# Row factor on VectorE, first low-rank split ahead of the key norm, token norm one unit later

## The chip, the cores and the metric

The kernel runs on one core of a Trainium2 chip. A core has a matrix engine (TensorE, PE in the profile; its weight loads are PEld), VectorE (DVE), ScalarE (ACT), GpSimd (POOL) and SyncE (SP), which here only issues transfers. Each takes its instructions in one order that is fixed when the program is built, and waits at an instruction until its semaphores are up. The metric is the device time of one execution in microseconds (us), as the median of several runs; lower is better. What is measured of this kernel without any change varies by some tenths of a per cent between runs.

## The reference, cut to what matters

One layer of a hybrid encoder in float32: 256 tokens, width 2048.

```python
u = rms_norm(x, norm_mix_pre)                # every token divided by its root mean square
proj = u @ w_in                              # q, k, v of two attentions, RWKV-7 inputs, gates
y_a = stick_breaking_attention(q_a, k_a, v_a)
y_b = forgetting_attention(q_b, k_b, v_b, log_f)
z = z + (z_prev - z) * mu                    # RWKV-7: token shift of the projected features
w_log = -softplus(-(w0 + tanh(wd) @ w_up)) - 0.5     # low-rank products with 64 rows
a = sigmoid(a0 + ad @ a_up)
kk = (k * k_k) / norm_of_each_head(k * k_k)          # the key norm
...                                          # recurrence over chunks of 64 tokens, group norm, gate
m = sum(sigmoid(gate_i) * (y_i @ P_i)); x = x + rms_norm(m @ w_out)
x = x + rms_norm(relu(rms_norm(x) @ w_mlp_up) ** 2 @ w_mlp_down)
```

The division by a token's root mean square is a factor per row of `u`, so `u @ w_in` may be formed without it and each result multiplied by the factor afterwards. The kernel does that.

## The kernel before, in words

**Weights.** All big weights lie in HBM as one stream of half-megabyte pieces. For each piece SP issues a transfer into a tile `raw` (three buffers); ACT copies it, rounded, to `whi` (L152); DVE subtracts to get the remainder `wlo` (L153). `wnext` keeps one piece ahead of the products (`AHEAD = 1`), and `whi` and `wlo` have three buffers each. A `raw` buffer comes free for the next transfer when DVE has made `wlo` from it.

**Units.** `unit(pks)` forms 128 columns of `u @ w_in` for all 256 tokens: two halves, each with eight products with `whi` (L168; the very last is L176) and eight with `wlo` (L172). The result stands in a PSUM bank in two parts. `evac` empties it: ACT copies one part (L227), DVE adds the other (L228). For RWKV features `shift` does the same with L585 and L586, and then mixes neighbouring tokens: ACT scales into `zp` (L588), DVE combines (L589). In `tok`, which forms 512 columns for 128 tokens at a time, the products are L198 and L214.

**The row factor.** `squares` sums the squares of the input into two tiles `a` (ACT L371, DVE L373). `norm` adds them over partitions with products with a matrix of ones (L378), and DVE and ACT make the factor `rstd` from that (L380, L241 to L246). `scaled(d)` multiplies a result by `rstd` (L395), in `evac`'s loop for the first eight units, after `evac` for the next eight, and inside `shift`. `turned_rstd` makes the same factor with tokens on partitions (L387 to L392).

**Mixers.** The attentions and RWKV run as generators between the products: a `yield` hands back control until a planned time of the written PE order has come, so their few products are written into PE's order at a planned place. PE's order is exactly this written one. The other engines' order is set by a scheduler when the program is built, from the order in which the code is written and what each instruction depends on; `pin` keeps one instruction where the code has it.

**Stick-breaking attention** (`sb_mix`) multiplies its logs by a mask on POOL (L448, two groups of four), ACT then rounds them (L454), and DVE takes the remainder (L455).

**RWKV, one half of the heads at a time** (`rwkv_half`): the squares of the keys (ACT L655, L660, DVE L661), sums per head on PE (L668), the inverse root (ACT L672, L675, DVE L670, L680 to L685; this is the key norm), then for each pair of heads `p` the low-rank products (PE L696). Their weights come through `lora_load(p)` (two transfers on ACT's queue, L639, into the one buffer `lor`) and `lora_split(p)` (ACT L645, then twice DVE L647, into the one tile `lows`).

In the second half of the heads the group norm and gate of the first half run at the same time (`gate_norm`: ACT L947, DVE L946, L948, L954, PE L952).

Of the kernel before, what the change touches and what calls it, by code (L numbers as in the profile page):

```python
# [12 lines left out]
AF = mybir.ActivationFunctionType  # L13
ALU = mybir.AluOpType
# [36 lines left out]
def hybrid_block(ctx, tc, xt, x, gains, params, consts, lora, gup, wst, out):  # L51
    nc = tc.nc
    V, A, G, PE = nc.vector, nc.scalar, nc.gpsimd, nc.tensor
# [11 lines left out]
    def nm(s):  # L65
        uid[0] += 1
        return f"{s}_{uid[0]}"
# [110 lines left out]
    def unit(pks):  # L178

        ps = gps()  # L180
        for h in range(2):
            hi, lo = wnext()
            gemm(ps, hi, lo, pks[8 * h:8 * h + 8], h == 0, h == 1, tick)
        return ps
# [37 lines left out]
    def pin(ins):  # L222
        return tc.keep_in_program_order(ins)

    def evac(ps, dst):
        b = tmp()
        A.activation(b, ps[:, T:2 * T], AF.Copy)  # L227
        V.tensor_tensor(dst, ps[:, 0:T], b, ALU.add)  # L228
# [25 lines left out]
    def g1(w=T):  # L254
        return rp.tile([128, T], F32, tag="g1", name=nm("g1"), bufs=20)
# [109 lines left out]
    rstd = rp.tile([128, T], F32, name="rstd1")  # L365
# [9 lines left out]
    def norm():  # L375
        ps = mps()
        for i in range(2):
            PE.matmul(ps[:, 0:T], C("ones"), A6[:, i, :], start=i == 0, stop=i == 1)  # L378
        ms, t = tmp(), tmp()
        V.tensor_scalar(ms, ps[:, 0:T], 1.0 / D, EPS, ALU.mult, ALU.add)  # L380
        rsqrt(rstd, ms, t)
        return ms

    def turned_rstd(ms):
        ps = mps()
        for tt in range(2):
            PE.matmul(ps[:, 4 * tt:4 * tt + 4], ms[0:4, tt * 128:tt * 128 + 128], C("ident", slice(0, 4), 0, 4),  # L387
                      start=tt == 0, stop=tt == 1)
        r8 = rt.rearrange("p a b -> p (a b)")
        V.tensor_copy(r8, ps[:, 0:8])  # L390
        G.tensor_tensor(r8, r8, cst[:, 2:3].to_broadcast([128, 8]), ALU.pow)
        V.tensor_scalar(rt[:, :, 1], rt[:, :, 0], 0.5, None, ALU.mult)  # L392

    def scaled(d):
        G.tensor_tensor(d, d, rstd[0:d.shape[0]], ALU.mult)  # L395

    for i in range(2):
        wsplit(wraw())
# [5 lines left out]
    for h in range(8):  # L404
        ps = qb[h] if h < 3 else unit(upk)
        qk.append(g1())
        evac(ps, qk[h])
        if h == 3:
            ms = norm()
        if h == 5:  # L410
            turned_rstd(ms)
        for i in range(h + 1) if h == 3 else [h] if h > 3 else []:
            scaled(qk[i])
    done["sbq"], done["sbk"] = qk[:4], qk[4:]

# [164 lines left out]
    def shift(ps, i, dst, n=128):  # L580

        b, t = tmp(), tmp()
        zp = rp.tile([128, T + 1], F32, tag="zp", name=nm("zp"), bufs=2)
        G.memset(zp[:, 0:1], 0.0)
        A.activation(b[0:n], ps[0:n, T:2 * T], AF.Copy)  # L585
        V.tensor_tensor(t[0:n], ps[0:n, 0:T], b[0:n], ALU.add)  # L586
        scaled(t[0:n])
        A.activation(zp[0:n, 1:T + 1], t[0:n], AF.Copy, scale=P("mu", i, slice(0, n)))  # L588
        V.scalar_tensor_tensor(dst, t[0:n], omu[0:n, i:i + 1], zp[0:n, 0:T], ALU.mult, ALU.add)  # L589
# [37 lines left out]
    def rwkv_half(hf):  # L627
        PR = range(4 * hf, 4 * hf + 4)
        xw, xa, wl = done["low"]
# [12 lines left out]
        def lora_split(p):  # L642
            if p in PR:
                raw = lor[p]
                pin(A.activation(wl, raw, AF.Copy))  # L645
                for i, r in enumerate((slice(64, 128), slice(0, 64))):
                    V.tensor_tensor(wl[r, i], raw[r, i], wl[r, i].bitcast(F32), ALU.subtract)  # L647

# [8 lines left out]
        for i2 in range(2):  # L657
            s = B6[:, 2 * i2:2 * i2 + 2, :]
            hl = [rp.tile([128, 2, T], F32R, tag="BK", name=nm("sqh"), bufs=8) for _ in range(2)]
            A.activation(hl[0], s, AF.Copy)  # L660
            V.tensor_tensor(hl[1], s, hl[0].bitcast(F32), ALU.subtract)  # L661
            sqh.append(hl)
        yield 3.8
        for i2 in range(2):
            ri = B6[:, 2 * i2:2 * i2 + 2, :]
# [20 lines left out]
            yield 3.0  # L686
        SC = rp.tile([128, 32, 128], F32, tag="SC", name=nm("SC"), bufs=1)
        At, Bt, Kt, bon = {}, {}, {}, {}
        lora_split(PR[0])
        ecol = rp.tile([128, 4, 4], F32, tag="ecol", name=nm("ecol"), bufs=2)  # L690
        for i, p in enumerate(PR):
            ps = mps()
# [41 lines left out]
            A.activation(kph, kp, AF.Copy)  # L734
            V.tensor_tensor(kpl, kp, kph.bitcast(F32), ALU.subtract)
            lora_split(p + 1)
            yield f"v{p}"
            v = done[f"v{p}"]
# [220 lines left out]
    def mixers():  # L959
        yield from sb_mix()  # L960
        yield from fox_mix()
        yield from rwkv_lora()
        for hf in range(2):
            yield from rwkv_half(hf)
# [36 lines left out]
    for s in ("q", "k"):  # L1001
        lst = []
        for h in range(4):
            ps = unit(upk)
            t = g1()
            evac(ps, t)
            scaled(t)
            lst.append(t)
        done["fox" + s] = lst
# [7 lines left out]
    for hf in range(2):  # L1017
        for s, mo in (("k", MU_K), ("r", MU_R), ("v", MU_V)):
            for p in range(4 * hf, 4 * hf + 4):
                ps = unit(upk)  # L1020
                d = g1()
# [634 lines left out]
```

## Time and profile before

| | us |
|---|---|
| median of 3 runs | 1519.44 |
| lowest, highest | 1519.37, 1525.15 |
| the profiled execution, its own time | 1523.08 |
| its span in the trace | 1521.3 |
| PE busy in it | 1489.9 |
| DVE, ACT, POOL busy in it | 1210.3, 937.7, 139.2 |

Times in the profile count from the start of the span. "Busy" is the time in which an engine has an instruction in work; behind a waiting instruction the profile names what ended the wait. The granted clock is the share of its full clock that PE was given, 1.00 or less, and stands in the views by stretches of time as PEclk. The profiled execution took 3.64 us more than the median of the runs.

The three stages that the change touches all lie in the first 545 us: the first eight units (to 58 us), the rest of the projections with the two attentions and the first half of RWKV (to 345 us), and the second half of RWKV (around 490 us). The feed-forward layer after that (about 840 us to the end) is not touched.

### The profile page before, as it was taken

The page shows a single profiled execution, that of the slowest core. Times are in us where ns is not written, and L with a number is a line of the kernel's source. Part 1 is how long each engine was busy: PE and PEld are TensorE (multiplying, and loading weights), DVE is VectorE, ACT ScalarE, POOL GpSimd, SP SyncE. Part 2 cuts the span into 40 slices and gives each one's busy share as a digit, 9 for nine tenths or more (in the row PEclk, how much of TensorE's full clock was granted, in tenths as well). Part 3 has the DMA queues.
Part 4 walks back from the last instruction along what each step waited for, and adds up shares of the span by engine and source line. Part 5 has one row for each costly group of instructions (what it writes and reads, how often), then busy time and mean ns, then how long its engine had stood idle before and what let it go on. Part 6 is the DMA issues. An engine that isn't in the chain of part 4 may idle for free.

```text
span 1521.3 us, 22774 instructions
## 1 busy us (share of the span) xinstructions
PE 1489.9 (98%) x8401; PEld 1253.3 (82%) x8401; DVE 1210.3 (80%) x1644; ACT 937.7 (62%) x1398; POOL 139.2 (9%) x203
## 2 busy tenths in 40 slices
PE   8999999999998999999999999999999999999997
PEld 7888887888777888778887888888888888888885
DVE  7566577779768789658655788989899999899986
ACT  7465666554557554565444676777677676676763
POOL 0232011320000100000000000000000000000000
PEclk9999999999999999999999999999999999999999
DMA  7545454444634545545695568788888888988874
GB/s 257 185 146 179 170 179 158 160 161 167 206 136 146 172 160 193 175 145 180 238 302 190 201 201 251 245 246 258 263 249 232 259 256 240 272 249 252 274 250 151
DMA packets 107616, 317.71 MB, mean 209 GB/s; under 512 B 10736, under 2 KB 14704, under 8 KB 107248
## 3 DMA queue, kind: packets, MB, share of 16 engines
q1 hardware_dynamic: 94832, 284.91, 54.4%
q0 software_dynamic: 8064, 29.36, 10.3%
q10 hardware_dynamic: 4608, 1.97, 0.5%
q8 instruction: 66, 1.08, 0.3%
q14 instruction: 46, 0.38, 0.1%
HBM read 282.65 MB, written 4.19 MB: 189 GB/s over the span
## 4 chain that ended last, share of the span: by engine, by line
PE 64%; DVE 2%; issue 1%; DMA 1%; ACT 1%; POOL 0%; POOLq 0%; DVEq 0%; ACTq 0%
PE gps L214 18%; PE gps L168 14%; PE gps L172 8%; PE gps L198 5%; PE mps L1386 3%; PE mps L1388 3%; PE mps L1387 3%; PE gps L1388 2%; PE gps L1386 2%; PE gps L1387 2%; PE gps L176 1%; DVE wlo L153 1%; DMA sp<-in_wst_dram 1%; PE mps L745 0%; ACT whi L152 0%
## 5 line engine op out<-in xcount | busy, mean ns | idle before, releaser
L153 DVE TENSOR_TENSOR wlo<-raw,whi 128x1024 fp32r<-128x1024 f32 x501 | 613.3, 1232 | 169.5 <-ACT whi L152 158.2
L152 ACT ACTIVATE whi<-raw 128x1024 fp32r<-128x1024 f32 x501 | 527.1, 1056 | 251.9 <-PE gps L214 113.1
L168 PE MATMUL gps<-pk,whi 128*128 128x512 f32 x1366 | 348.2, 394 | 2.2 <-ACT whi L152 2.1
L168 PEld LDWEIGHTS gps<-pk,whi 128*128 128x128 f32 x1366 | 254.2, 190 | 52.6 <-ACT whi L152 2.4
L214 PE MATMUL gps<-whi,pk 128*128 128x512 f32 x1144 | 288.9, 392 | 0.0
L214 PEld LDWEIGHTS gps<-whi,pk 128*128 128x128 f32 x1144 | 212.6, 188 | 44.3
L172 PEld LDWEIGHTS gps<-pk,wlo 128*128 128x128 f32 x1456 | 200.3, 192 | 14.4 <-DVE wlo L153 0.2
L172 PE MATMUL gps<-pk,wlo 128*128 128x256 f32 x1456 | 205.4, 284 | 0.0
L214 PE MATMUL gps<-wlo,pk 128*128 128x512 f32 x572 | 156.0, 392 | 0.3 <-DVE wlo L153 0.3
L214 PEld LDWEIGHTS gps<-wlo,pk 128*128 128x128 f32 x572 | 106.3, 188 | 23.2 <-DVE wlo L153 1.1
L1252 DVE TENSOR_TENSOR sp<-raw,sp 128x1024 fp32r<-128x1024 f32 x67 | 81.7, 1219 | 3.3 <-ACT sp L1251 3.1
L1278 ACT ACTIVATE sp<-gps 128x512 f32<-128x512 f32 x52 | 31.1, 598 | 82.9 <-PE gps L176 82.9
L1251 ACT ACTIVATE sp<-raw 128x1024 fp32r<-128x1024 f32 x67 | 70.6, 1053 | 13.6 <-PE mps L1387 4.7
L1348 POOL DMA_DIRECT2D raw<-raw x40 | 34.9, 873 | 426.2 <-DVE raw L1345 121.3
L198 PE MATMUL gps<-whi,pk 128*128 128x512 f32 x264 | 72.0, 394 | 0.0
L1386 PE MATMUL mps<-whi,fm 128*128 128x512 f32 x168 | 66.1, 394 | 0.0
L1388 PE MATMUL mps<-wlo,fm 128*128 128x512 f32 x168 | 65.7, 391 | 0.4 <-DVE wlo L153 0.2
L1387 PE MATMUL mps<-whi,fm 128*128 128x512 f32 x168 | 65.8, 392 | 0.0
L198 PEld LDWEIGHTS gps<-whi,pk 128*128 128x128 f32 x264 | 49.6, 190 | 10.5 <-ACT whi L152 0.2
L1388 PE MATMUL gps<-wlo,fm 128*128 128x512 f32 x126 | 49.2, 391 | 0.4 <-DVE wlo L153 0.4
L1386 PE MATMUL gps<-whi,fm 128*128 128x512 f32 x126 | 49.2, 391 | 0.0
L1345 DVE TENSOR_TENSOR raw<-raw,raw 128x1024 f32<-128x1024 f32 x40 | 48.8, 1220 | 0.4
(378 smaller groups left out, 1997.8 us busy)
## 6 DMA issues: line engine op xcount, KB each, us to landing
raw<-in_wst_dram SPq DMA_DIRECT2D x499, 512.0 KB, 4.3
raw<-raw POOLq DMA_DIRECT2D x40, 512.0 KB, 6.7
sp<-in_wst_dram SPq DMA_DIRECT2D x16, 512.0 KB, 5.8
raw<-sp POOLq DMA_DIRECT2D x8, 512.0 KB, 6.6
sp<-raw POOLq DMA_DIRECT2D x8, 512.0 KB, 8.5
x<-in_x_dram SPq DMA_DIRECT2D x8, 256.0 KB, 5.2
xs<-x SPq DMA_DIRECT2D x2, 1024.0 KB, 3.9
x<-xs SPq DMA_DIRECT2D x4, 512.0 KB, 6.0
```

Of the source, the lines that this page charges most:

```text
L152: A.activation(hi, raw, AF.Copy)
L153: V.tensor_tensor(lo, raw, hi.bitcast(F32), ALU.subtract)
L168: PE.matmul(ps, hi[:, i * 128:i * 128 + 128], pks[i], start=first and i == 0, stop=False)
L172: PE.matmul(ps[:, 0:T], lo[:, i * 128:i * 128 + 128], pks[i][:, 0:T], start=False, stop=False)
L198: PE.matmul(ps[tt], pks[k][:, c:c + 128], w[:, (k - k0) * 512:(k - k0) * 512 + 512], start=k == 0 and part == 0 and w is hl[0], stop=w is ...
L214: PE.matmul(ps[tt], pks[k][:, c:c + 128], w[:, (k - k0) * 512:(k - k0) * 512 + 512], start=k == 0 and part == 0 and w is hl[0], stop=False)
L1251: A.activation(hi, raw, AF.Copy)
L1252: V.tensor_tensor(lo, raw, hi.bitcast(F32), ALU.subtract)
L1345: V.tensor_tensor(x, x, z, ALU.add)
L1386: PE.matmul(Q[f], p, w, start=d == 0 and i == 0, stop=False)
L1387: PE.matmul(Q[f], pl, w, start=False, stop=False)
L1388: PE.matmul(Q[f], p, wl, start=False, stop=d == nd - 1 and i == 1)
```

## The change

```diff
     def scaled(d):
-        G.tensor_tensor(d, d, rstd[0:d.shape[0]], ALU.mult)
+        V.tensor_tensor(d, d, rstd[0:d.shape[0]], ALU.mult)
...
         evac(ps, qk[h])
-        if h == 3:
+        if h == 4:
             ms = norm()
-        if h == 5:
+        if h == 6:
             turned_rstd(ms)
-        for i in range(h + 1) if h == 3 else [h] if h > 3 else []:
+        for i in range(h + 1) if h == 4 else [h] if h > 4 else []:
             scaled(qk[i])
...
         def lora_split(p):
             if p in PR:
                 raw = lor[p]
-                pin(A.activation(wl, raw, AF.Copy))
+                A.activation(wl, raw, AF.Copy)
                 for i, r in enumerate((slice(64, 128), slice(0, 64))):
                     V.tensor_tensor(wl[r, i], raw[r, i], wl[r, i].bitcast(F32), ALU.subtract)
...
             sqh.append(hl)
+        lora_split(PR[0])
         yield 3.8
...
         At, Bt, Kt, bon = {}, {}, {}, {}
-        lora_split(PR[0])
```

The multiplication by `rstd` goes from POOL (`G`) to DVE (`V`), 43 times: 16 whole results of `evac`, 27 times in `shift`. The products with ones of `norm` are written one unit later, behind the fifth unit instead of the fourth, and those of `turned_rstd` behind the seventh. The split of the first pair's low-rank weights is written ahead of the key norm, and the ACT copy of every such split may now be moved by the scheduler.

**POOL and ACT in the stick-breaking attention.** `sbt` holds the logs, `sbh` their rounded copy, `g_146` and `g_155` are results of units, `whi_993` is the piece that the unit after next begins with. POOL, before:

```order
L448 TENSOR_TENSOR sbt<-sbt,con 128x128 x4
L395 TENSOR_TENSOR g_146_897<-g_146_897,rstd_310 128x256
L448 TENSOR_TENSOR sbt<-sbt,con 128x128 x4
L395 TENSOR_TENSOR g_155_957<-g_155_957,rstd_310 128x256
```

POOL, after:

```order
L448 TENSOR_TENSOR sbt<-sbt,con 128x128 x8
```

The second group of masks no longer stands behind a multiplication. On ACT at the same place, before:

```order
L152 ACTIVATE whi_937<-raw_935 128x1024
L152 ACTIVATE whi_965<-raw_963 128x1024
L454 ACTIVATE sbh<-sbt 128x768 x2
L227 ACTIVATE tmp_958<-gps_902 128x256
L152 ACTIVATE whi_993<-raw_991 128x1024
```

ACT, after:

```order
L152 ACTIVATE whi_937<-raw_935 128x1024
L454 ACTIVATE sbh<-sbt 128x768
L152 ACTIVATE whi_965<-raw_963 128x1024
L454 ACTIVATE sbh<-sbt 128x768
L227 ACTIVATE tmp_958<-gps_902 128x256
L152 ACTIVATE whi_993<-raw_991 128x1024
```

One L454 now stands ahead of `whi_965`; `whi_993` still stands behind both.

**DVE at the first low-rank split.** `lor_2272` holds the weights of pair 0; `g_285` is the first key, `g_442` a later unit's result. DVE, before, at the end of the key norm:

```order
L685 TENSOR_TENSOR b_399_2271<-b_399_2271 128x512
L153 TENSOR_TENSOR wlo_2524<-raw_2521,whi_2523 128x1024
L589 SCALAR_TENSOR_TENSOR g_442_2488<-tmp_2490,omu,zp_2491 128x256
L647 TENSOR_TENSOR lows<-lor_2272,lows 64x128 x2
L153 TENSOR_TENSOR wlo_2583<-raw_2580,whi_2582 128x1024
```

DVE, after, some 75 us earlier in the program, behind the first key:

```order
L395 TENSOR_TENSOR tmp_1686<-tmp_1686,rstd_310 128x256
L153 TENSOR_TENSOR wlo_1753<-raw_1750,whi_1752 128x1024
L589 SCALAR_TENSOR_TENSOR g_285_1684<-tmp_1686,omu,zp_1687 128x256
L647 TENSOR_TENSOR lows<-lor_2272,lows 64x128 x2
L586 TENSOR_TENSOR tmp_1741<-gps_1694,tmp_1740 128x256
```

The split no longer stands behind the key norm. In the second half of the heads it moves likewise (`lor_4518`). DVE there, before:

```order
L685 TENSOR_TENSOR b_815_4517<-b_815_4517 128x512
L948 TENSOR_TENSOR g_756_4075<-g_756_4075,g_599_3169 128x256
L647 TENSOR_TENSOR lows<-lor_4518,lows 64x128
L954 TENSOR_TENSOR g_756_4075<-mps_4820,g_756_4075 128x256
L647 TENSOR_TENSOR lows<-lor_4518,lows 64x128
```

DVE, after, inside the last pair of the first half:

```order
L705 SCALAR_TENSOR_TENSOR cs_3215<-con,lw_3214 128x256
L715 TENSOR_TENSOR g_617_3255<-g_617_3255,g_320_1876 128x256
L647 TENSOR_TENSOR lows<-lor_4518,lows 64x128 x2
L717 SCALAR_TENSOR_TENSOR kkr_3258<-g_320_1876,par,b_399_2271 128x256
L718 SCALAR_TENSOR_TENSOR tha_3216<-tha_3216,lw_3214 128x256
```

It now runs some 160 us before it is needed, as soon as the products of pair 3 have read the tile `lows`.

## The prediction

> **What bounds the kernel now.** I read the page first, then PE's waits, then the granted clock in narrow stretches round each wait, then the timeline at each place. The page's head says that PE sets the pace:
>
> ```profile
> span 1521.3 us, 22774 instructions
> PE 1489.9 (98%) x8401; PEld 1253.3 (82%) x8401; DVE 1210.3 (80%) x1644; ACT 937.7 (62%) x1398; POOL 139.2 (9%) x203
> ```
>
> PE is idle for 1521.3 - 1489.9 = 31.4 us, so work on other engines costs time only where PE waits for it. Of PE's list of waits, five lines (line, what released it, total, times, longest):
>
> ```profile
> PE mps L696 <- DVE lows L647: 6.3, 2, 3.3
> PE gps L198 <- DVE wlo L153: 2.3, 1, 2.3
> PE gps L168 <- ACT whi L152: 2.1, 1, 2.1
> PE mps L378 <- DVE a L373: 2.1, 1, 2.1
> PE mps L1162 <- DVE x L1130: 1.9, 1, 1.9
> ```
>
> The first four are 12.8 us, all before 500 us; the fifth is the only one over 0.5 us after that. Busy time hides a second loss: how fast PE runs. In a table by stretch the columns are the stretch, then busy us of PE, PEld, DVE, ACT and POOL with counts, then PEclk, DMA share and GB/s:
>
> ```profile
> 33.50:36.90 3.40, 2.26 (x10) 1.95 (x11) 2.89 (x5) 1.46 (x3) 0.00 (x0) 1.00 0.82 267
> 108.60:112.00 3.40, 3.40 (x14) 2.90 (x13) 3.40 (x4) 2.03 (x4) 1.90 (x2) 0.50 0.56 166
> 262.20:265.60 3.40, 2.22 (x7) 2.02 (x8) 2.42 (x5) 0.78 (x3) 0.10 (x1) 0.50 0.47 166
> 265.60:269.00 3.40, 3.40 (x13) 3.03 (x12) 0.69 (x1) 0.70 (x3) 0.00 (x0) 0.50 0.58 186
> 487.50:490.90 3.40, 0.45 (x2) 0.17 (x2) 3.34 (x8) 1.17 (x2) 0.00 (x0) 0.50 0.62 195
> 490.90:494.30 3.40, 3.40 (x12) 3.03 (x13) 2.25 (x5) 1.80 (x4) 0.00 (x0) 0.50 0.51 167
> ```
>
> After three of the waits the clock stands at 0.50 for one or two stretches of 3.4 us, in which half of PE's busy time is lost. After the wait at 32.6 it stays at 1.00. So a wait removed returns its idle time and may return up to 1.7 us for each half-clock stretch.
>
> **The change, term by term, against the profiled execution (1523.08, span 1521.3).**
>
> (a) Norm one unit later.
>
> ```profile
> 33.90 0.68 DVE L373 TENSOR_TENSOR a<-a 128x512 f32<-128x512 f32 x1
> 34.64 1.13 PE L378 MATMUL mps<-a,con 128*128 128x256 f32 x4 [2.06 <-DVE a L373]
> ```
>
> The sum of squares ends at 34.58 and PE has waited 2.06 us for it. One unit later PE comes at about 38, past that. Gain 2.06; nothing less, since PE has a whole unit ready to run instead.
> The cover of the moved rest: `rstd` comes a unit later, and six multiplications then stand in a row on DVE. At 0.42 us each (row in (e)) that is 2.5 us ahead of one `wlo`. The pieces are made about a half unit ahead, 259.42 - 256.63 = 2.79 us by these rows of PE at full clock, so I take 0 and keep 0 to 2.5 us of loss.
>
> ```profile
> 256.63 2.00 PE L168 MATMUL gps<-pk,whi 128*128 128x512 f32 x8
> 259.42 0.63 PE L168 MATMUL gps<-pk,whi 128*128 128x512 f32 x2
> ```
>
> (b) POOL without the multiplications. PE's wait for `whi` is this chain:
>
> ```profile
> 97.99 4.41 POOL L448 TENSOR_TENSOR sbt<-sbt,con 128x128 f32<-128x128 f32 x4 [5.65 <-DVE sbt L445]
> 102.36 0.74 POOL L395 TENSOR_TENSOR g<-g,rstd 128x256 f32<-128x256 f32 x1
> 102.43 0.85 ACT L454 ACTIVATE sbh<-sbt 128x768 fp32r<-128x768 f32 x1 [3.54 <-POOL sbt L448]
> 103.06 2.48 POOL L448 TENSOR_TENSOR sbt<-sbt,con 128x128 f32<-128x128 f32 x4
> 105.57 0.84 ACT L454 ACTIVATE sbh<-sbt 128x768 fp32r<-128x768 f32 x1 [2.30 <-POOL sbt L448]
> 107.69 3.00 PE L168 MATMUL gps<-pk,whi 128*128 128x512 f32 x8 [2.12 <-ACT whi L152]
> ```
>
> ACT sits at L454 until the masks are done, and behind L454 stand the next evacuation and the `whi` that PE needs. Without L395 the second group starts 103.06 - 102.36 = 0.70 us earlier. The first group waits for L445, which in DVE's new order has one L444 and one piece less ahead of it and one L589 more; I estimate 1.2 us. The second L454 then ends about 1.9 us earlier, at 104.5 instead of 106.4, and PE's wait shrinks to a few tenths. The half-clock stretch behind it (3.40 us busy, 1.70 lost) then has no cause. Full gain 2.12 + 1.70 = 3.8; none if the masks run as late as now on a busier DVE. I take 3.0, nearer the full end, because both the first and second group lose something ahead of them.
>
> (c) The first split of half 0.
>
> ```profile
> 258.80 0.41 ACT L645 ACTIVATE lows<-lor 128x256 fp32r<-128x256 f32 x1
> 262.95 0.60 DVE L647 TENSOR_TENSOR lows<-lor,lows 64x128 fp32r<-64x128 f32 x2
> 263.38 0.98 PE L696 MATMUL mps<-lows 128*128 128x256 f32 x3 [3.33 <-DVE lows L647]
> ```
>
> L647 stands behind the key norm and the pieces on a DVE that has no gap there, so PE waits 3.33 us. Moved some 75 us ahead it is done long before. Its weights are there too:
>
> ```profile
> L639 ACTq DMA_DIRECT2D lor<-in_lora_dram x16: 602/626/723, 182.5 to 520.5; - x16
> DMA to landing us min/median/max: 2.4/2.5/5.1
> 184.37 2.15 ACT L152 ACTIVATE whi<-raw 128x1024 fp32r<-128x1024 f32 x2
> ```
>
> The first transfer is issued at 182.5, and L645's new place is behind the two `whi` that end at 186.5; a landing as late as 5.1 would hold ACT for about 2 us there, off PE's path as long as a piece is ready. The transfers of the next pair are issued earlier on ACT's queue, 0.63 us each as before; SP's queue is unchanged and POOL's only gets shorter. Gain: 3.33 idle, and half of the busy 2.22 + 3.40 us in the two half-clock stretches, 2.81: together 6.1. At least 3.33 - 2 = 1.3, if the pieces that follow are late next (PE used this wait to let DVE catch up).
>
> (d) The first split of half 1. Two waits stand close together:
>
> ```profile
> 487.00 0.81 PE L198 MATMUL gps<-wlo,pk 128*128 128x512 f32 x2 [2.33 <-DVE wlo L153]
> 490.76 1.14 PE L696 MATMUL mps<-lows 128*128 128x256 f32 x3 [2.95 <-DVE lows L647]
> ```
>
> The split goes, so 2.95 goes. The wait of 2.33 for `wlo` is DVE's gate and key norm, which the change does not touch there; it stays. It alone can bring one half-clock stretch, now with PE at work in it. Clock lost now: half of 0.45 + 3.40, 1.9; then 1.7. Gain 2.95 + 0.2 = 3.2; up to 4.9 if the clock stays full.
>
> (e) The price. DVE has no such instruction now; the nearest has its shape and two inputs, L586, and POOL's own stands beside it (line, busy, mean ns):
>
> ```profile
> L586 DVE TENSOR_TENSOR tmp<-gps,tmp 128x256 f32<-128x256 f32 x26 | 10.9, 418 | 9.8 <-ACT tmp L585 9.7
> L395 POOL TENSOR_TENSOR tmp<-tmp,rstd 128x256 f32<-128x256 f32 x26 | 30.9, 1190 | 111.2 <-DVE tmp L586 105.0 <-DVE foxsm L549 6.2
> 320.00:342.00 22.00, 21.30 (x127) 17.34 (x125) 18.17 (x27) 12.32 (x23) 5.65 (x11) 1.00 0.48 164
> 332.14 0.91 POOL L395 TENSOR_TENSOR tmp<-tmp,rstd 128x256 f32<-128x256 f32 x1 [0.87 <-DVE tmp L586]
> 332.38 1.76 DVE L153 TENSOR_TENSOR wlo<-raw,whi 128x1024 fp32r<-128x1024 f32 x1
> 334.19 1.20 PE L214 MATMUL gps<-wlo,pk 128*128 128x512 f32 x4
> L153 DVE TENSOR_TENSOR wlo<-raw,whi 128x1024 fp32r<-128x1024 f32 x501 | 613.3, 1232 | 169.5 <-ACT whi L152 158.2
> 341.54 0.33 PE L771 MATMUL mps<-con,g 64*64 64x64 f32 x4 [0.57 <-DVE SC L755]
> ```
>
> 43 x 0.418 = 18.0 us more on DVE, about 0.42 per unit of some 5.6 us. Elsewhere pieces have slack; at 320 to 342 DVE is busy 18.17 of 22.00, and PE takes `wlo` 0.05 us after it is made (332.38 + 1.76 = 334.14, used at 334.19). There one multiplication (0.42) and the moved pair L647 (0.60) come ahead of that piece, and the piece itself gets shorter when POOL no longer runs beside it (1.76 against a mean of 1.23, 0.5 back). Net about 0.5, and 0.1 more at L771. I take 0.6. Bounds: a gain of 0.5, if only the shortening counts; a loss of 2.5, four units' multiplications (1.7) plus the pair and L771.
>
> Sum: 2.06 + 3.0 + 6.1 + 3.2 - 0.6 = 13.8, so 1523.08 - 13.8 = 1509.3 for an execution like the profiled one. That one is 3.64 us over the median of 1519.44. If the difference is only the profiler's, the median becomes 1505.6. If it is two half-clock stretches (2 x 1.7 = 3.4) that the other runs didn't have, they can't be given back, and it is 1509.3. I take the middle, 1507.4. Nothing later takes the gain back: of PE's waits only the 1.9 us at L1162 lie there.
>
> **The rivals.** About 0.5% (7.6 us, below 1511.8 or above 1527.0) can be told from no change.
> 1. Only idle time returns, because half-clock stretches depend on where a wait falls and not on its length: 2.06 us at 32.6 cost no clock, 2.12 us at 105.6 did. For: the spread of the runs. Idle alone: 2.06 + 1.9 + 3.33 + 2.95 - 0.6 = 9.6, so about 1509.8, still faster. The Trainium skill, "TensorE: Matmul & The Clock Gate", section "HAM oscillation", sets its limit at idle gaps of about 3.4 us; by that no wait here would slow the clock and the sum would be these 9.6 us. The trace differs: 0.50 right behind a wait of 2.12. The page does say that the window runs freely, which is this rival.
> 2. The waits move on: in the key norm's stage DVE is without gaps, and PE, now earlier, waits for `wlo` instead of the split. Terms (c) and (e) shrink to 1.3 and -2.5, (b) to 1: 2.06 + 1 + 1.3 + 3.2 - 2.5 = 5.1, so about 1514.4: no change that can be told. Against: behind that wait PE's list shows no other for `wlo` until 320 us, so DVE has some lead there.
> 3. Slower: between 264 and 342 DVE falls behind for good. Each of 14 units then pays 0.42 of wait and gathers enough idle for a half-clock stretch, 1.7: 14 x 2.1 = 29.7, less 13.8, so about 1535. It decides at the point where DVE's work in that stage exceeds PE's time; now it is 18.17 of 22.00 in the fullest part, and four units add 1.7.
> 4. The change doesn't do what it says: ACT's rounding still holds up `whi`, and the scheduler's new places bring waits of the same size. Then about 1519.
>
> **How the numbers follow.** Forecast 0.60, rival 1 0.18, rival 2 0.12, rival 3 0.05, rival 4 0.05. Faster is the forecast and most of rival 1: 0.77. Same is rivals 2 and 4 and the rest of 1: 0.18. Slower is rival 3: 0.05. The range's lower end takes the whole of the three removed waits and their clock: 2.06 + 3.8 + 6.1 + 4.9 = 16.9 off the median, 1502.5. Its upper end takes in rival 1 and goes towards rival 2: idle of (a), (c), (d), 8.3, less 2.5, is 5.8 off, 1513.6; I put 1513.5.
>
> **What would show it.** PE's waits no longer have L378 or L696; the wait for `whi` at L168 is under 0.6 us; the wait for `wlo` at L198 near 485 is still about 2.3. L395 stands on DVE with some 0.42 us, and L153's mean falls. The clock is 1.00 round 100 and 250 us. Wrong would be: new waits of PE at L172 or L214 for `wlo` between 40 and 345 us, or L168 still waiting 2 us behind L454.

## The result, and the profile after

| | us |
|---|---|
| changed kernel, median of 4 runs | 1504.78 (1503.62 to 1505.96) |
| kernel before, median of 4 runs beside it | 1520.65 (1519.37 to 1525.15) |
| ratio | 0.9890, 95% interval 0.9867 to 0.9913 |
| profiled execution after, its span | 1505.96, 1504.2 |

The change makes the kernel 1.1% faster. Forecast were 1507.4, range 1502.5 to 1513.5, faster with a chance of 0.77. The two profiled executions differ by 1523.08 - 1505.96 = 17.1 us, where the prediction's sum was 13.8.

The head of the page of the changed kernel:

```profile
span 1504.2 us, 22802 instructions
PE 1482.5 (99%) x8401; PEld 1247.0 (83%) x8401; DVE 1215.7 (81%) x1687; ACT 938.2 (62%) x1398; POOL 95.1 (6%) x160
```

DVE has 43 instructions more and POOL 43 less, as the change says. PE is idle for 21.7 us instead of 31.4 (9.7 less), and its busy time fell by 7.4 although it does the same 8401 products. Most of that is the clock: in the half-clock stretches near 108, 262 and 487 us of before, which the changed kernel doesn't have, PE lost half of 3.40, 5.62 and 3.85 us, 6.4 in all. PE's waits now (line, releaser, total, times, longest):

```profile
PE gps L198 <- DVE wlo L153: 2.3, 1, 2.3
PE mps L1162 <- DVE x L1130: 1.9, 1, 1.9
PE gps L1388 <- DVE wlo L153: 1.6, 2, 1.1
...
PE gps L168 <- ACT whi L152: 0.4, 1, 0.4
```

L378 and L696 are gone from the list, L168 has 0.4 left of 2.1, and L198 keeps its 2.3. At the three places where PE lost time, in the timeline of PE:

```profile
37.37 0.40 PE L176 MATMUL gps<-pk,whi 128*128 128x512 f32 x1
37.60 1.02 PE L378 MATMUL mps<-a,con 128*128 128x256 f32 x4
...
253.58 0.63 PE L168 MATMUL gps<-pk,whi 128*128 128x512 f32 x2
254.04 0.52 PE L696 MATMUL mps<-lows 128*128 128x256 f32 x3
...
472.40 0.73 PE L198 MATMUL gps<-wlo,pk 128*128 128x512 f32 x2 [2.34 <-DVE wlo L153]
472.98 0.52 PE L696 MATMUL mps<-lows 128*128 128x256 f32 x3
```

L378 and both first L696 start with no idle time ahead. The stretches that answer to those of before (PE, PEld, DVE, ACT, POOL, then the granted clock):

```profile
100.50:103.90 3.40, 3.40 (x19) 2.97 (x20) 3.40 (x5) 2.78 (x4) 0.00 (x0) 1.00 0.35 102
249.40:252.80 3.40, 3.40 (x21) 2.99 (x20) 3.40 (x6) 1.77 (x4) 0.10 (x1) 1.00 0.49 180
467.93:471.35 3.42, 2.13 (x10) 1.43 (x8) 3.36 (x10) 1.55 (x2) 1.02 (x2) 1.00 0.55 180
471.35:474.76 3.41, 2.36 (x14) 2.14 (x15) 3.41 (x6) 2.50 (x4) 0.00 (x0) 1.00 0.42 144
474.76:478.17 3.41, 3.41 (x17) 2.83 (x16) 3.41 (x7) 2.08 (x6) 0.00 (x0) 1.00 0.46 175
```

All at 1.00, also behind the wait of 2.34 that stayed.

**Where the time came from.** PE's order is the same in both programs but for the few products of `norm`. So the start of one and the same product in two traces tells how far PE is ahead. The table gives what PE gained (-) or lost (+) against the profiled execution of before in each stage, for the changed kernel and for the experiments below; the stages are cut at fixed products, named by their time in the trace of before. The first column (start-up, the same code in all) and the last two (output projections, feed-forward) are variation between executions. So are some entries between: where a run still has a wait of before, a half-clock stretch may follow it or not (section on the clock), as for e2_vector to 56 us, e3_split to 115 us and e1_norm to 274 us.

| us | to 20 | to 56 | to 115 | to 274 | to 394 | to 508 | to 844 | to the end | span |
|---|---|---|---|---|---|---|---|---|---|
| changed | -0.42 | -2.29 | -3.13 | -6.14 | -2.69 | -4.55 | -0.18 | +2.30 | -17.1 |
| e1_norm | -0.27 | -2.30 | -0.01 | -2.59 | 0.00 | +1.02 | +0.50 | +2.20 | -1.4 |
| e2_vector | -0.15 | +1.36 | -3.13 | -2.47 | -2.69 | +1.10 | +0.59 | -0.08 | -5.5 |
| e3_split | -0.71 | -0.02 | -1.59 | -5.73 | +0.51 | -3.37 | +0.53 | -1.38 | -11.8 |
| e4_half0 | -0.68 | -2.29 | -3.13 | -6.14 | -2.69 | -3.41 | -0.05 | -0.29 | -18.7 |
| e5_pinned | -0.62 | -2.30 | -3.14 | -6.14 | -2.69 | -3.68 | -0.33 | +0.13 | -18.8 |
| e9_beside | -0.41 | -2.29 | -2.68 | -6.14 | -2.19 | -3.46 | -0.15 | -1.40 | -18.7 |
| e10_twice | +0.33 | -2.29 | -2.80 | -6.13 | -2.30 | -4.37 | +0.02 | +0.91 | -16.6 |
| e11_gate4 | -0.65 | -2.29 | -3.14 | -6.14 | -2.69 | -4.27 | +0.18 | +0.76 | -18.3 |

### The profile page after: what moved, and what is told of

Read it like the earlier page. It is cut to its first block, busy times and chain, and to the rows that moved or that the text cites. A ratio compares the mean times of both kernels' runs of the same rounds, so it can differ in the third digit from the quotient of the medians.

```text
span 1504.2 us, 22802 instructions
## 1 busy us (share of the span) xinstructions
PE 1482.5 (99%) x8401; PEld 1247.0 (83%) x8401; DVE 1215.7 (81%) x1687; ACT 938.2 (62%) x1398; POOL 95.1 (6%) x160
## 3 DMA queue, kind: packets, MB, share of 16 engines
q8 instruction: 66, 1.08, 0.3%
## 4 chain that ended last, share of the span: by engine, by line
PE 61%; DMA 2%; issue 2%; DVE 2%; ACT 0%; POOL 0%; POOLq 0%; DVEq 0%; SPq 0%; ACTq 0%
PE gps L214 18%; PE gps L168 13%; PE gps L172 7%; PE gps L198 5%; PE mps L1386 3%; PE mps L1388 3%; PE mps L1387 3%; PE gps L1388 2%; PE gps L1386 2%; PE gps L1387 2%; DMA sp<-in_wst_dram 1%; DVE wlo L153 1%; PE gps L176 1%; DMA raw<-raw 1%; DMA raw<-in_wst_dram 1%
## 5 line engine op out<-in xcount | busy, mean ns | idle before, releaser
L168 PE MATMUL gps<-pk,whi 128*128 128x512 f32 x1366 | 345.9, 392 | 0.5 <-ACT whi L152 0.4
L168 PEld LDWEIGHTS gps<-pk,whi 128*128 128x128 f32 x1366 | 252.8, 188 | 50.4 <-ACT whi L152 0.6
L214 PE MATMUL gps<-whi,pk 128*128 128x512 f32 x1144 | 288.9, 392 | 0.0
L214 PEld LDWEIGHTS gps<-whi,pk 128*128 128x128 f32 x1144 | 212.6, 188 | 44.2
L214 PE MATMUL gps<-wlo,pk 128*128 128x512 f32 x572 | 155.9, 392 | 0.0
L214 PEld LDWEIGHTS gps<-wlo,pk 128*128 128x128 f32 x572 | 106.3, 188 | 22.9 <-DVE wlo L153 0.7
L1251 ACT ACTIVATE sp<-raw 128x1024 fp32r<-128x1024 f32 x67 | 70.6, 1054 | 16.6 <-PE mps L1387 5.0
L198 PE MATMUL gps<-whi,pk 128*128 128x512 f32 x264 | 71.2, 391 | 0.0
L198 PEld LDWEIGHTS gps<-whi,pk 128*128 128x128 f32 x264 | 49.1, 188 | 10.3 <-ACT whi L152 0.2
```

Of the source, the lines that this page charges most:

```text
L168: PE.matmul(ps, hi[:, i * 128:i * 128 + 128], pks[i], start=first and i == 0, stop=False)
L198: PE.matmul(ps[tt], pks[k][:, c:c + 128], w[:, (k - k0) * 512:(k - k0) * 512 + 512], start=k == 0 and part == 0 and w is hl[0], stop=w is ...
L214: PE.matmul(ps[tt], pks[k][:, c:c + 128], w[:, (k - k0) * 512:(k - k0) * 512 + 512], start=k == 0 and part == 0 and w is hl[0], stop=False)
L1251: A.activation(hi, raw, AF.Copy)
```

## The experiments

### One part alone: norm, vector, split

**e1_norm.**

```diff
-        if h == 3:
+        if h == 4:
             ms = norm()
-        if h == 5:
+        if h == 6:
             turned_rstd(ms)
-        for i in range(h + 1) if h == 3 else [h] if h > 3 else []:
+        for i in range(h + 1) if h == 4 else [h] if h > 4 else []:
```

> The kernel before with one part of the change alone: the products of norm one unit later. Theory A (each part acts at its own place, and the places add up): PE's wait of 2.06 us at L378 <- a goes, nothing else moves; PE reaches 55 us about 2.3 us earlier, and the time falls by 2.3 us (0.15%). Theory B (the parts help each other): without the multiplications on DVE a burst of six L395 stands on POOL in a row, at 0.73 us each 4.4 us, and holds the keys that the units after it need; then the gain is under 1 us, and the waits for whi at L168 (2.1), for lows at L696 (2 of 6.3 in all) and for wlo at L198 (2.3) stay in both.

Measured: 1518.75 us against 1522.62, ratio 0.9975 (0.9965 to 0.9986). At its own place it gains the 2.30 us that it gains in the changed kernel, so six multiplications in a row on POOL cost PE nothing there, and theory A stands for the place. But the stage to 274 us gained 2.59 too, with nothing changed there, and its wait at L696 is as long as before. PE's row and the two windows over which that wait lies, with the one behind it, in this kernel:

```profile
260.80 0.61 PE L696 MATMUL mps<-lows 128*128 128x256 f32 x3 [3.32 <-DVE lows L647]
...
255.73:259.14 3.41, 1.75 (x12) 1.27 (x10) 3.38 (x6) 1.75 (x4) 0.83 (x1) 1.00 0.47 163
259.14:262.56 3.42, 1.76 (x10) 1.58 (x11) 2.90 (x5) 0.80 (x2) 0.10 (x1) 1.00 0.41 138
262.56:265.97 3.41, 3.41 (x22) 3.04 (x21) 1.81 (x3) 3.12 (x8) 1.12 (x2) 1.00 0.61 210
```

A wait of 3.32 us, and the clock stays at 1.00. In the trace of before the same wait of 3.33 was followed by two stretches at 0.50. The section on the clock comes back to this.

**e2_vector.**

```diff
     def scaled(d):
-        G.tensor_tensor(d, d, rstd[0:d.shape[0]], ALU.mult)
+        V.tensor_tensor(d, d, rstd[0:d.shape[0]], ALU.mult)
```

> The kernel before with the multiplication by rstd on DVE alone. Theory A: it owns the gain of 3.0 us near 105 us (PE's wait for whi 2.1 goes to 0.4 or less, and the half-clock stretch behind it) and also the 2.5 to 2.9 us that PE gained between 318 and 390 us, because L153 no longer runs beside POOL: together 5.5 to 5.9 us less. Theory B: the gain between 318 and 390 us comes from the split (the pair L647 and its place in the scheduler's order), and this kernel gains 3.0 alone, or 2.4 with the loss of 0.6 that the prediction gave to the multiplications. The waits at L378 (2.06) and L696 (3.3 and 2.95) stay in both.

Measured: 1516.73 us, ratio 0.9964 (0.9951 to 0.9977), 5.9 us less. Theory A holds at both places: 3.13 us to 115 us and 2.69 from 274 to 394 us, to the hundredth what the changed kernel has there. The prediction had the second of them as a loss.

**e3_split.**

```diff
-                pin(A.activation(wl, raw, AF.Copy))
+                A.activation(wl, raw, AF.Copy)
...
+        lora_split(PR[0])
         yield 3.8
...
         At, Bt, Kt, bon = {}, {}, {}, {}
-        lora_split(PR[0])
```

> The kernel before with the first split of each half moved ahead of the key norm, and the splits' ACT copy free to be moved; POOL still multiplies, norm stays. Theory A: 6.0 us gained near 263 us and 4.7 near 490 us, nothing between 318 and 390: 10.7 us less. Theory B (the split owns the gain at 318 to 390 us too): 13.2 to 13.6 us less. Theory C (PE runs into the next late wlo, since DVE's lead at 263 us was bought by the wait): 1.3 + 3.2, 4.5 us less.

Measured: 1514.97 us (1511.30 to 1517.42), ratio 0.9955 (0.9939 to 0.9970), 7.7 us less in the median; the profiled execution is the fastest of its runs. In it 5.73 us come from the stage to 274 us and 3.37 from the one to 508 us, and nothing from 274 to 394. Another 1.59 come from the stage to 115 us, where nothing is changed: the wait of 2.09 us at L168 is still there, but PE was busy 1.86 us of the window 105.37 to 108.78 and the clock stayed at 1.00. B is out; C is out too, since PE met no late piece behind 263 us. The median lies between A and C, the runs spread over 6 us (those of the kernel before over 6.5), and the parts by place are read from one execution.

The three medians add up to 3.9 + 5.9 + 7.7 = 17.5 us, against 17.2 for the three together (e4_half0 below). By place they don't: to 274 us they give 2.59 + 2.47 + 5.73 = 10.8, where only 6.14 are to be had.

### Which half of the split's edit does it

**e4_half0.**

```diff
-        lora_split(PR[0])
+        if PR[0] == 0:
+            lora_split(PR[0])
         yield 3.8
...
         At, Bt, Kt, bon = {}, {}, {}, {}
+        if PR[0]:
+            lora_split(PR[0])
```

> The changed kernel, with the first split moved ahead for half 0 alone; in half 1 it stands behind the key norm again. Tells the term of half 1 by itself. Theory A: slower than the changed kernel by 4.7 us (the wait of 2.95 us at L696 is back, and with the wait of 2.3 for wlo close to it the half-clock stretch of 1.7 us too), so about 11 us faster than before. Theory B (the half clock depends on where a wait falls, and the place is now 14 us earlier): the wait of 2.95 is back, the clock stays at 1.00, and it is slower than the changed kernel by 3.0, so 13 us faster than before.

Measured: 1505.39 us (1504.00 to 1506.96), ratio 0.9888 (0.9873 to 0.9904). Both theories fell: no wait at L696, and no slower than the changed kernel. The built program shows why: its instructions stand in the same order on every engine as the changed kernel's. Once the ACT copy isn't pinned, the scheduler takes it forward to the earliest place by itself, wherever the split is written. The same holds for e3_split: with the copy freed and the split left where it was, the program is the same. So this run is a repeat of the changed kernel, and the measure of how well times agree: 0.6 us.

**e5_pinned.** The other half of the edit alone: written ahead of the key norm, but pinned.

```diff
-                A.activation(wl, raw, AF.Copy)
+                pin(A.activation(wl, raw, AF.Copy))
```

> The changed kernel with the ACT copy of every low-rank split held in program order again; the first split of each half stays written ahead of the key norm. Runs so far: freeing the copy, with the split written where it was, gives the same program as the changed kernel on every engine. Theory A (either edit takes the split off the key norm's queue): no wait of PE at L696 and the time of the changed kernel, 1505, within 1.5 us. Theory B (freeing the copies of the other six pairs is what matters too, since it reorders L731, L589 and the pieces between 300 and 390 us): the two waits at L696 go, but 1 to 3 us slower than the changed kernel, lost between 300 and 390 us.

Measured: 1505.84 us (1504.28 to 1506.10), ratio 0.9898 (0.9877 to 0.9918). Theory A: each half alone is enough, and the copies of the other six pairs give nothing (-2.69 from 274 to 394 us with them and without). It gains less to 508 us (-3.68) because of a new wait of 0.97 us at L876 near 435 us, where the changed kernel waits 0.3.

### Why the multiplication gained where it was to cost

The trace of before had the answer. ACT's and DVE's waits in it, over the whole span:

```profile
ACT zp L588 <- POOL tmp L395: 27.3, 24, 3.6
DVE g L589 <- ACT zp L588: 8.7, 8, 1.2
```

The same of the changed kernel:

```profile
ACT zp L588 <- DVE tmp L395: 2.6, 5, 1.3
DVE g L589 <- ACT zp L588: 0.2, 1, 0.2
```

And one unit near 323 us of before, in the timelines of POOL, ACT and DVE:

```profile
323.58 1.65 POOL L395 TENSOR_TENSOR tmp<-tmp,rstd 128x256 f32<-128x256 f32 x1 [3.47 <-DVE tmp L586]
...
325.27 0.52 ACT L588 ACTIVATE zp<-tmp,par 128x256 f32<-128x256 f32 x1 [2.70 <-POOL tmp L395]
325.69 1.04 ACT L152 ACTIVATE whi<-raw 128x1024 fp32r<-128x1024 f32 x1
...
326.76 1.23 DVE L153 TENSOR_TENSOR wlo<-raw,whi 128x1024 fp32r<-128x1024 f32 x1 [0.46 <-ACT whi L152]
```

POOL takes 1.65 us; ACT stands at L588 for 2.70 until it is done; the `whi` of the next piece is behind L588 on ACT, and the `wlo` behind that. A whole unit's multiplication stood in the pieces' way. The same unit after the change, DVE and ACT (the changed kernel's PE is about 12 us ahead there):

```profile
308.94 0.42 DVE L586 TENSOR_TENSOR tmp<-gps,tmp 128x256 f32<-128x256 f32 x1 [1.30 <-ACT tmp L585]
309.40 0.42 DVE L395 TENSOR_TENSOR tmp<-tmp,rstd 128x256 f32<-128x256 f32 x1
...
309.92 0.51 ACT L588 ACTIVATE zp<-tmp,par 128x256 f32<-128x256 f32 x1
310.62 1.06 ACT L152 ACTIVATE whi<-raw 128x1024 fp32r<-128x1024 f32 x1 [0.19 <-PE mps L696]
```

L586 ends at 309.36 and that `whi` starts 1.3 us later; before, L586 ended at 323.50 and the `whi` started 2.2 us later. What reaches PE of this is small at each unit. PE's waits from 265 to 395 us of before, of which the changed kernel has none:

```profile
PE mps L771 <- DVE SC L755: 0.6, 1, 0.6
PE gps L214 <- DVE wlo L153: 0.3, 1, 0.3
PE mps L771 <- ACT Kt L758: 0.2, 1, 0.2
```

L755 stands behind such a `wlo` on DVE. Comparing the starts of the same products, PE gains 1.1 us at L771 near 342 us of before, 0.6 at L214 near 353, and the rest of the 2.69 in steps of 0.2 or less between 318 and 385 us.

Two runs tell this chain from the other candidate, DVE's instructions stretched by POOL beside them, and from luck with DVE's room.

**e9_beside** (line numbers behind 397 are 3 higher in this kernel and the next):

```diff
+    spent = cpool.tile([128, 192], F32, name="spent")
+
     def scaled(d):
         V.tensor_tensor(d, d, rstd[0:d.shape[0]], ALU.mult)
+        G.tensor_tensor(spent[0:d.shape[0]], d[:, 0:192], rstd[0:d.shape[0], 0:192], ALU.mult)
```

> The changed kernel, and after each of the 43 multiplications on DVE one more on POOL into a tile that nobody reads (192 of the 256 columns, since there is no room for more). DVE's, ACT's and PE's order is that of the changed kernel; on POOL one of the new instructions stands between the two groups of masks L448, as the multiplication did before. Theory A (the 2.7 us that PE gained between 318 and 390 us come from DVE's instructions no longer being stretched by POOL beside them): they are lost again, the pieces L153 beside POOL take up to 1.8 us, and near 100 us up to 3.0 us are lost too: 3 to 6 us slower than the changed kernel. Theory B (they come from POOL's long way between L586 and L588 being gone): nothing lost between 318 and 390 us, 0 to 3.0 us near 100 us: 0 to 3 us slower.

Measured: 1506.30 us (1504.38 to 1507.04), ratio 0.9895 (0.9877 to 0.9912), 0.9 us over e4_half0. The group of the new instruction:

```profile
L398 POOL TENSOR_TENSOR spent<-tmp,rstd 128x192 f32<-128x192 f32 x26 | 39.1, 1502 | 115.4 <-DVE tmp L397 109.2 <-DVE foxsm L552 6.2
L153 DVE TENSOR_TENSOR wlo<-raw,whi 128x1024 fp32r<-128x1024 f32 x501 | 611.3, 1228 | 160.4 <-ACT whi L152 149.6 <-PE gps L214 3.2 <-ACT gn L923 2.2
```

POOL works beside DVE as before and even longer, 1502 ns each, but nobody waits for it, and PE keeps 2.19 of the 2.69 us from 274 to 394 and 2.68 of 3.13 to 115. The 0.5 us from 274 to 394 are lost at one `wlo` that comes 0.19 us late near 268 us, ahead of the places where the 2.69 were gained; those it keeps in full. So POOL's work beside DVE costs about 0.5 us at each of two places in this run, but its absence doesn't explain the gain from 318 to 385 us. By exclusion and by the rows above that gain goes to the chain: theory B.

One thing is left open. The edit also changes the order that the scheduler makes. With the vector part alone ACT and DVE keep their order in that stage but for one piece near 279 us and one unit near 333 us, whose L588 and L589 now stand behind the next `whi` and `wlo` instead of ahead. Either way the piece no longer waits for the multiplication, but no run tells how much of the 2.69 us is the shorter way and how much this new place.

**e10_twice**: the same line with `V` for `G`.

> The changed kernel with the same extra 43 multiplications (192 of 256 columns, into a tile that nobody reads) on DVE: about 0.33 us each, 14 us more work for DVE. Measures the price of the multiplications by itself. Theory A (DVE has room, the extra work costs PE nothing except where DVE runs without gaps): 0 to 2 us slower than the changed kernel, lost at 2 or 3 places (near 35 to 58 us, 300 to 345 us). Theory B (DVE was at its limit there and only luck of the order hid the first 18 us): each of some 14 units between 240 and 345 us pays 0.33 and more, 5 us or more slower.

Measured: 1506.00 us (1504.12 to 1506.41), ratio 0.9890 (0.9873 to 0.9908). In the list of groups (busy, mean ns):

```profile
L398 DVE TENSOR_TENSOR spent<-tmp,rstd 128x192 f32<-128x192 f32 (+1 forms) x27 | 10.0, 372 | 0.4
...
L398 DVE TENSOR_TENSOR spent<-g,rstd 128x192 f32<-128x192 f32 x16 | 5.8, 364 | 0.2
```

10.0 + 5.8 = 15.8 us more on DVE cost PE 0.33 + 0.01 + 0.39 + 0.18 = 0.9 us in the four stages from 56 to 508 us. Theory A: DVE had room for the multiplications twice over.

### The wait that stayed

**e6_gate4, e7_gate5, e11_gate4.** DVE is nearly without a gap from 464.6 us on (busy 7.67 of the 7.80 us to 472.4), with `gate_norm` of the first half and the key norm of the second together. These spread the gate.

```diff
-            yield 2.0 if hf else 2.8
+            yield 2.0 if hf else 4.0     # e7_gate5: 5.5
         mark(f"gn{hf}")
```

> The changed kernel with the gate of the first half of the heads spread wider beside the key norm of the second: 4.0 instead of 2.8 us of planned PE time per pair. Theory A (the wait of 2.34 us for wlo at L198 near 470 us is DVE's load in that place alone): the wait shrinks below 1 us and the span falls by about 1.5 to 2.3 us, and by up to 1.7 more where that wait had a half-clock stretch behind it. Theory B (ACT is late there, because whi stands behind L947, and DVE only follows): the wait stays at about 2.3.

> The same with 5.5 us per pair, so that two of the four gates stand behind the key norm. Theory A: the wait for wlo at L198 near 470 us is gone (2.3 us less). Theory B: it stays, or comes back a few us later, since the gates' five instructions per pair meet the first pair of the second half instead.

Measured, one execution each: 1503.68 and 1505.98 us. PE's row of that wait with 4.0, and the wait that came behind it:

```profile
471.60 0.73 PE L198 MATMUL gps<-wlo,pk 128*128 128x512 f32 x2 [1.37 <-DVE wlo L153]
...
480.70 2.11 PE L214 MATMUL gps<-whi,pk 128*128 128x512 f32 x8 [0.57 <-ACT whi L152]
```

Half of A: the wait shrank by 0.97, and by 481 us PE was level with the changed kernel again. With 5.5 the wait for `wlo` is down to 0.30 and others took its place (1.7 for `whi` at L214, 0.9 at L751). Timed:

> The changed kernel with the gate of the first half spread to 4.0 us per pair, timed. Its first look: the wait for wlo at L198 went from 2.34 to 1.37 us, and a new wait of 0.57 for whi at L214 came 9 us later, so that PE was level again. Theory A (only the clock can gain: a wait of 1.37 cannot fill more than half a window of 3.41 us, so no half-clock stretch follows it in any execution, as one of 1.7 us does behind a wait of 2.3 in some): 0 to 1.7 us faster than the changed kernel, about 0.8, at the edge of what can be measured. Theory B: the same time as the changed kernel, 1505.

Measured: 1505.03 us (1504.05 to 1505.35), ratio 0.9885 (0.9868 to 0.9902). That is the time of the changed kernel (1504.78 and 1505.39). Spreading the gate moved the wait and gained nothing that can be told.

Why that place stays short isn't shown. Theory B has support that these runs leave untouched: just ahead of its stretch without gaps DVE stood still for 3.05 us, more than PE's wait of 2.34, for ACT's L947 (3.06 in e6_gate4, the same). ACT and DVE in the changed kernel, where L673 and L676 are the key norm's L672 and L675 of before:

```profile
459.22 1.28 ACT L673 ACT_TABLE_LOAD   x1
...
461.17 1.28 ACT L676 ACT_TABLE_LOAD   x1
...
463.95 0.58 ACT L947 ACTIVATE g<-g,par 128x256 f32<-128x256 f32 x1
...
464.57 0.43 DVE L948 TENSOR_TENSOR g<-g,g 128x256 f32<-128x256 f32 x1 [3.05 <-ACT g L947]
```

ACT makes such a table load of 1.28 us ahead of each L673 and L676, four between 453 and 463 us, and the gate's L947 stands behind them. No run takes these loads away, so what they cost PE is open.

### The clock

e4_half0 has the program of the changed kernel and the same wait near 470 us. PE's row and the windows of e4_half0:

```profile
472.05 0.88 PE L198 MATMUL gps<-wlo,pk 128*128 128x512 f32 x2 [2.33 <-DVE wlo L153]
...
469.07:472.48 3.41, 1.08 (x5) 0.57 (x4) 3.38 (x7) 1.60 (x2) 1.02 (x2) 1.00 0.41 148
472.48:475.89 3.41, 3.41 (x14) 3.02 (x13) 3.41 (x8) 2.48 (x6) 0.00 (x0) 0.50 0.58 183
```

The same 2.3 us as in the changed kernel, and now a half-clock stretch, in which 3.41/2 = 1.7 us are lost. Set against the changed kernel, PE falls back by 1.56 us over it and regains 0.34 by 485 us, where a `wlo` is no longer late. The difference is where the wait falls. The edges of the half-clock stretches of one trace lie on a grid of 3.41 us. Here the wait (469.72 to 472.05) lies in one window: PE busy 1.08 of 3.41. In the changed kernel the grid's edge at 471.35 cuts the wait in two, PE is busy 2.13 and 2.36 of the two windows, and nothing happens. In e1_norm 3.32 us were cut into 1.67 and 1.65. So it was with the wait of 2.06 us at L378 before the change, which cost no clock: it was cut into 0.95 and 1.11. In e2_vector that wait (1.84 us) lay in one window, and a half-clock stretch followed at 35.62.

**e8_pauses** makes waits on purpose:

```diff
+    again = dict(zip(range(205, 300, 8), (3, 4, 4, 5, 4, 3, 4, 4, 5, 4, 4, 3)))
+    nsplit = [0]
...
         A.activation(hi, raw, AF.Copy)
-        V.tensor_tensor(lo, raw, hi.bitcast(F32), ALU.subtract)
+        for _ in range(1 + again.get(nsplit[0], 0)):
+            V.tensor_tensor(lo, raw, hi.bitcast(F32), ALU.subtract)
+        nsplit[0] += 1
```

> A probe of the clock: at 12 pieces between about 550 and 830 us the subtraction L153 is done 3 to 5 times more than needed (1.22 us each), so that PE waits for wlo at chosen places; everything else is the changed kernel. Theory A (length rule): the half-clock stretch follows every wait of 2.1 us or more and no wait under 1.8. Theory B (windows): in a grid of 3.41 us that starts at the edges of the half-clock stretches, a stretch at 0.50 follows each window in which PE was idle for more than about 1.8 us and no window with less than about 1.65, whatever the length of the wait: a wait of 2.3 us cut by an edge into two parts gives none, and one of 3 us gives one. Some waits fall on either side.

Measured: 1529.46 us, one execution. Most pauses hid behind PE's work; the windows with the largest idle time, each with the one behind it:

```profile
668.78:672.19 3.41, 1.54 (x8) 0.94 (x6) 3.41 (x4) 0.08 (x1) 0.00 (x0) 1.00 0.00 0
672.19:675.60 3.41, 3.41 (x12) 2.83 (x11) 3.35 (x8) 1.45 (x3) 0.00 (x0) 0.50 0.69 192
...
692.67:696.09 3.42, 2.35 (x11) 1.64 (x10) 3.42 (x5) 1.24 (x2) 0.00 (x0) 1.00 0.00 0
696.09:699.50 3.41, 3.20 (x18) 2.65 (x19) 3.41 (x7) 1.21 (x4) 0.00 (x0) 1.00 0.02 5
...
747.28:750.70 3.42, 0.00 (x0) 0.00 (x0) 3.39 (x4) 0.00 (x0) 0.00 (x0) 1.00 0.81 250
750.70:754.11 3.41, 1.28 (x3) 1.09 (x4) 2.04 (x2) 1.06 (x1) 0.00 (x0) 0.50 0.81 272
```

Half clock behind 1.87 us idle (3.41 - 1.54) and behind a window idle throughout, none behind 1.07. The probe gave too few waits round the threshold to decide alone; all profiled executions together do (last section). Against theory A, the length of the wait, e1_norm's 3.32 us without a half-clock stretch already speaks.

## Why the prediction was right, and where it was wrong

| term | predicted | measured | verdict |
|---|---|---|---|
| (a) norm later | 2.06 | 2.29; 2.30 alone | right |
| (b) `whi` at L168 | 3.0 | 3.13; 3.13 with the vector part alone | right sum, one step wrong |
| (c) first split, half 0 | 6.1 | 6.14 | right |
| (d) first split, half 1 | 3.2 | 4.55 here; 3.41 in a repeat | its upper end here, the clock |
| (e) price on DVE | -0.6 | +2.69 | wrong sign |

Sum of the terms: 13.8 predicted, 18.8 measured. Start-up and the stage to 844 us add 0.6 and the feed-forward takes 2.3 back, so 17.1 for the two executions.

(a) PE comes to L378 at 37.60 behind a whole unit, without a wait. The burst of six multiplications cost PE nothing, on POOL (e1_norm) or on DVE.

(b) The prediction said that the second group of masks would start 0.70 us earlier since no multiplication stands between the groups, and that the first gains 1.2 from DVE's order. In the changed kernel:

```profile
92.80 7.43 POOL L448 TENSOR_TENSOR sbt<-sbt,con 128x128 f32<-128x128 f32 x8 [0.79 <-DVE sbt L445]
...
98.59 0.85 ACT L454 ACTIVATE sbh<-sbt 128x768 fp32r<-128x768 f32 x1 [3.83 <-POOL sbt L448]
99.34 1.04 ACT L152 ACTIVATE whi<-raw 128x1024 fp32r<-128x1024 f32 x1
...
100.44 1.88 PE L168 MATMUL gps<-pk,whi 128*128 128x512 f32 x7 [0.38 <-ACT whi L152]
```

The masks start at 92.80 instead of 97.99; 2.7 of that PE had gained already, 2.5 come from L445's place on DVE, twice the estimate. The gap between the groups doesn't matter: e9_beside has a POOL instruction in it again and PE waits the same 0.4 us, because the `whi` that it waits for now stands between the two L454, behind the first. It is another piece than before, and PE didn't wait for it then: this new wait is why the gain is 3.13 and not the full 3.8.

(c) went as worked out, idle time and clock. That it is all due to the split's place on DVE holds only in part: with the vector part alone, 1.4 us of this wait and a half-clock stretch went too (L696 waits 4.9 us in all instead of 6.3).

(d) The wait of 2.95 went and the one of 2.33 stayed, as said. A half-clock stretch behind the latter came in the repeat (-3.41) and not in the profiled execution (-4.55); the difference is 1.1 us rather than 1.7, since PE regained part of it. Both ends had been named.

(e) is the step that failed. It counted 18 us of new work on DVE and its neighbours' shorter time, and looked at what POOL's and DVE's instructions cost each other and PE. It did not follow the chain to which L395 belongs: DVE L586, POOL L395, ACT L588, and the piece's `whi` behind L588. ACT's list of waits, which the prediction doesn't use, has 27.3 us there. e10_twice prices the work itself at 0.4 us in that stage, and e9_beside shows that the stretching isn't what was gained from 318 us on; what is left is the chain, with the new order of one unit in it.

The median was taken between two ends, for the case that the profiled execution of before had two half-clock stretches more than the rest. Over 17 runs the median of before is 1522.62, so that execution (1523.08) was an ordinary one. That the time lies in the range is in part luck: the change is worth 17.2 us against the 17 runs (e4_half0), more than the 16.9 of the range's lower end. The time stayed above that end because the range was counted from 1519.44, the median of three runs, which lies 3.2 us below that of the 17.

Rival 1 had the mechanism right (a half-clock stretch hangs on where a wait falls) and the consequence wrong: the clock lost at the three places came back, and PE's busy time fell by 7.4 us. Rivals 2 and 3 did not come: PE waits for no `wlo` over 0.2 us between 265 and 395 us, nor does it with the work doubled. Rival 4 is true of one line of the diff: writing the split earlier changes nothing once its copy is free.

## What to carry to other kernels

An operation that is handed from one engine to another and back costs what stands behind the waiting instruction on the third engine, not its own duration; read the waits of every engine on the chain, not those of the bottleneck alone. Before an edit that moves code is costed, look at the built order with each half of the edit alone: here a copy pinned behind the key norm was the whole cause, and either half removed it. When two heavy pieces of side work meet in one place, spreading one of them may only move the wait, as here; look first at what the full engine waited for just before.

## What the runs showed of the hardware

The granted clock goes to 0.50 for one window of 3.41 us, sometimes two, after a window of that length in which PE was idle for about half; the grid runs on by itself, so that the same program pays or not from one execution to the next. Over the 13 profiled executions, between 60 and 1480 us, 24 windows at full clock had PE idle for 1.84 us or more, and 23 were followed by 0.50 (the exception, in e10_twice, had 1.94); of 23 windows with 0.9 to 1.7 us, one was (1.36); of 3 between, one. A window already at 0.50 was followed by another one in all 5 cases in which PE was idle for 0.88 us or more of it, and by 1.00 in all 25 with 0.35 or less; so the wait of 3.33 of before, with 2.17 us in one window and 1.16 in the next, brought two. The Trainium skill, "TensorE: Matmul & The Clock Gate", section "HAM oscillation", speaks of idle gaps over about 3.4 us; here 1.8 us inside one window were enough, and 3.32 us across two were not.

A multiplication of 128x256 takes 0.42 us on DVE and took 1.19 on POOL on average, and up to 1.65 in the rows above beside a busy DVE.
